# A hybrid diffusion backbone: six pre-norm columns, five staging buffers and another DMA queue in the S5 front, and the first pre-norm pair of the feed-forward stages evacuated ahead of the normed rows

## The chip, the cores and the metric

The kernel runs on one core of a Trainium2 chip. The metric is the device time of one execution in microseconds (us). All other times are read from one execution that the hardware profiler recorded: its span runs from the first to the last instruction, and every time of day below counts from the start of that span.

## What is computed

One inference step of a backbone with two layers over 384 tokens (128 context tokens and 256 latents) of width 1024. A layer is a feed-forward block, a token mixer and another feed-forward block; each sub-layer is modulated by the conditioning and closed by a residual sum and a layer norm:

```
h   = x * (1 + scale) + shift                      # per sub-layer, from the conditioning
ffn = (silu(g) * a) @ w_down,  a, g = split(h @ w_up)      # D_FF = 2816
x   = layer_norm(ALPHA * x + w * gate * sublayer(h))       # w = 1/2 for ffn, 1 for a mixer

s5:  u = h @ w_in;  per group of 16 channels a diagonal complex state of 64, scanned
     forwards and backwards;  y = C s + d_skip * u;  out = a * sigmoid(g) of gelu(y) @ w_glu
```

The mixer of layer 0 is S5, that of layer 1 an RG-LRU block. So there are six sub-layers, numbered 0 to 5: feed-forward (0), S5 (1), feed-forward (2, 3), RG-LRU (4), feed-forward (5).

## The kernel before

Activations are held transposed: 128 channels on the partitions, 384 tokens along the free axis, eight such rows `r[:, k]`. All large products are made in float32 out of rounded parts: a weight tile (`raw`, 128x1024, loaded on the sync engine's queue, SP) is split into `hi` on ScalarE (L252) and `lo` on VectorE (L255), activations likewise into `hh` (L315) and `hl` (L316), and `mm3` (L261) adds three matmuls. Weight tiles have seven buffers, `hi` and `lo` five each, and products six PSUM banks.

**Starting ahead of the norm.** `Norm.add` (L346) gathers the sums of a row and at once writes the row, scaled but not yet normed, to `ph` and `pl`. The next sub-layer begins its products on these "pre-norm" rows. `Norm.pre` (L367) runs them in groups: in the first group, at step k = 4 of 8, TensorE sums the statistics (`stats`, L380), from which GpSimd works out mean and reciprocal deviation in some twenty tiny operations (L394 to L411); in the second group, at step `self.late`, `spread` (L414) broadcasts them with TensorE into `rs` and `ms`. `self.late` is 6 where the sub-layer that was normed is number 1, 2 or 4, that is for the three feed-forward stages 2, 3 and 5, and otherwise 4. Then `pre` loads the weights for what follows and calls `rest` (L425): for each k two operations on VectorE norm the row (L429, L430), `modulate` makes `hh` and `hl` of it, and GpSimd prepares the residual (L432). Everything after that uses normed rows. A product made of pre-norm rows is corrected when it leaves PSUM, by `apply` (L452): a copy of four columns (L455), a product with `rs` (L457) and two additions of `ms` terms (L459).

**Feed-forward** (`ffn`, L467). With a previous norm, the first three pairs (a value and a gate half each, so two PSUM banks a pair, six in all) are pre-norm. They are evacuated by `evac_pre` (L489) after `rest`, in order of the program; the fourth pair is the first on normed rows and needs two of the six banks.

**S5 front** (`s5`, L793). `proj` (L813) makes u = h @ w_in in eight columns of 128 channels. Columns 0 to 3 are pre-norm, in two groups of two; columns 4 to 7 come from normed rows. Each column is corrected, written to a staging buffer `s5stg` (three buffers; VectorE writes the context part, L829, ScalarE the latents, L831 or L833, GpSimd zeroes a separator, L822) and sent to DRAM as `ud` by a DMA on GpSimd's queue (L834), in runs of 49 floats. After every second column two more DMAs on that queue fetch the two columns back into `U` (L838), now with time and channel on the partitions. Columns 4 to 7 are in a part in which GpSimd's work keeps the order of the program.

**What uses U.** `inputs(b)` (L852), for 16 blocks of four groups, multiplies U with the tables `etd` (L864); blocks 2m and 2m + 1 need column m. ScalarE and VectorE copy the results to `s5sb` (L850, L870, L871). The scan (`steps`, L873) is 32 rounds of four small operations (L881 to L884) in three blocks of groups: 0 to 23 on VectorE (needs blocks up to 5), 24 to 39 on GpSimd (up to 9) and 40 to 63 on VectorE, begun after 22 rounds of the first (needs all 16). After it `align` (L894), the output products (L920), a way through DRAM and back into a staging buffer (`fetch`, L927), and the gated projection.

Outside the parts in manual order, the framework orders each engine's work by priority, which is the order of the program, and lets later work that is ready go first where earlier work is not.

Of the kernel before, what the change touches and what calls it, by code (L numbers as in the profile page):

```python
# [7 lines left out]
F32 = mybir.dt.float32  # L8
# [10 lines left out]
N = NP + NS  # L19
# [4 lines left out]
Q = 8  # L24
NC_ = 49
ADA_BUFS = 3
ADA_VEC = [(0, 2, 2)] + [(1, s, kind) for s in range(3) for kind in range(3)]
NX = N + 4
# [5 lines left out]
SK = 0  # L34
ADAS = 4, 2
COLS = ((0, NP, 0), (NP, N, 1))

# [7 lines left out]
def backbone(ctx, tc, a, o):  # L45
    nc = tc.nc
# [237 lines left out]
    def load_singles(srcs):  # L284
        return [stream(src, 1024) for src in srcs]
# [38 lines left out]
    class Norm:  # L324
# [3 lines left out]
        def __init__(self, i):  # L328
# [3 lines left out]
            self.last = []  # L332
            self.late = 6 if i in (1, 2, 4) else 4
            self.st = ExitStack()
# [31 lines left out]

        def pre(self, load, group, srcs, n, then):  # L367


            srcs = [srcs[j:j + n] for j in range(0, len(srcs), n)]  # L370
            w, ps = [load(srcs[0])], []
            for j in range(len(srcs)):
                if j + 1 < len(srcs):
                    w.append(load(srcs[j + 1]))
                ps = ps + group(w[j], NX, self.ph, self.pl, {0: {4: self.stats}, 1: {self.late: self.spread}}.get(j, {}))
            nxt = load(then)
            self.rest()
            return ps, nxt
# [88 lines left out]
    def ffn(i, splits, prev, side, before_last=None, first=None):  # L467
# [31 lines left out]
        with ExitStack() as st:  # L499
            f0 = 0  # L500
            up = lambda f: a["up"][l, s, f]
            for si, nf in enumerate(splits):
                zs.clear()
                f = f0
                if si == 0:
# [6 lines left out]
                    else:  # L512
                        zp = phase(st, f"z{i}")
                        f = 3
                        pss, w = prev.pre(load_pairs, pairs, [up(j) for j in range(f)], 1, [up(f)])
                        for ps in pss:
                            evac_pre(*ps)
# [275 lines left out]
    def s5(i, prev):  # L793
        l, s3 = divmod(i, 3)
        with ExitStack() as st:
# [8 lines left out]
            def stage():  # L804
                return sa.tile([128, Q, NC_], F32, name="s5stg", tag="stg", bufs=3)

# [3 lines left out]
            sin = lambda m: a["s5in"][m // 2, :, (m % 2) * 1024:(m % 2) * 1024 + 1024]  # L810
            nxt = [None]

            def proj(h, pre, before_last=None):  # L813
                if pre:
                    ps, nxt[0] = prev.pre(load_singles, singles, [sin(j) for j in range(4)], 2, [sin(4), sin(5)])
                    nxt.append(load_singles([sin(6), sin(7)]))
                else:
                    ps = singles(nxt[0], N, hh, hl) + singles(nxt[1], N, hh, hl)
                for m in range(4 * h, 4 * h + 4):
                    j = m % 4  # L820
                    stg = stage()
                    G.memset(stg[:, :, 16:17], 0.0)  # L822
                    if pre:
                        t, b = prev.apply(ps[j])
                    else:
                        t, b = ps[j], (0.0, None)
                    inp = t[:, 0:128].rearrange("p (c t) -> p t c", t=Q)
# [4 lines left out]
                    else:  # L832
                        S.activation(stg[:, :, 17:49], ins, AF.Copy)  # L833
                    nc.gpsimd.dma_start(by_channel(ud, m), stg)  # L834
                    if m == 4 * h + 3 and before_last is not None:
                        before_last()
                    for q in ((m - 1, m) if m % 2 else ()):
                        nc.gpsimd.dma_start(U[:, q * 8:q * 8 + 8, :].rearrange("p g c -> p (g c)"), by_place(ud, q))  # L838

            proj(0, True)  # L840
            prev.close()
            with ExitStack() as st2:
# [89 lines left out]
                with tc.manual_schedule(engines={ET.Pool}):  # L932
                    proj(1, False, al_tiles)
                    with tc.manual_schedule(engines={ET.DVE, ET.Activation, ET.SP}):
# [129 lines left out]
    def lru(i, prev):  # L1064
# [88 lines left out]

        ps, w = prev.pre(load_singles, singles, [lin(j) for j in range(4)], 2, [lin(j) for j in range(4, 8)])
        raw = lambda m: fetched(lin(m) if m < 16 else lout(m - 16), 1024)
# [268 lines left out]
```

## Time and profile before

| | us |
|---|---|
| median of 3 runs | 1648.69 (1647.26 to 1650.11) |
| the profiled execution | 1647.38 |
| its span | 1645.6 |
| TensorE busy in the span | 1550.3 (94%) |
| VectorE | 1277.0 (78%) |
| ScalarE | 706.7 (43%) |
| GpSimd | 348.6 (21%) |
| mean granted clock of TensorE | 0.972 of full speed |

PE is TensorE's matmuls and PEld its weight loads, DVE is VectorE, ACT ScalarE, POOL GpSimd, SP the sync engine; a q behind a name is the engine's sequencer or queue. An instruction is named by its line, its operation and "out<-in". Matmuls overlap, so a single one shows about 0.34 us although one ends every 0.175 us or so. Busy shares say how much work an engine has, not what ends last.

### The profile page before, as it was taken

Reading aid. Unit: us, or ns where it says so; the run is one execution under the profiler, and the core shown is the slowest. Engines: PE = TensorE matmul, PEld = TensorE weight load, DVE = VectorE, ACT = ScalarE, POOL = GpSimd, SP = SyncE. Lnnn points to the kernel's source line nnn. Section 1 sums busy time; section 2 is a strip of 40 time slices with the busy share of each in tenths; the row PEclk is TensorE's granted clock in tenths of the full one; section 3 lists DMA queues with packets and bytes.
Section 4 is the critical chain, followed back from the end, with each engine's and each line's share of the span. In section 5 each row is a group of like instructions: output and inputs, shape, how many; then the busy total and the mean of one; then the engine's idle time right before and its main releaser. Section 6 shows DMA issues by size and latency. Waiting matters only on the chain.

```text
span 1645.6 us, 25849 instructions
## 1 busy us (share of the span) xinstructions
PE 1550.3 (94%) x9554; PEld 1475.7 (90%) x9554; DVE 1277.0 (78%) x2742; ACT 706.7 (43%) x1157; POOL 348.6 (21%) x532
## 2 busy tenths in 40 slices
PE   7989999999888999999999999999989599999996
PEld 5877887889877999999999899999977599999995
DVE  4999999977586568968778998977797989644444
ACT  4422332345455456333335533334569366333332
POOL 0145445423562004000001400000155422000001
PEclk9989999999999999999999999999999899999997
DMA  9766777877487642757556266755514143544321
GB/s 351 255 221 213 232 247 233 261 242 262 97 265 239 226 152 79 239 178 247 185 156 223 88 212 201 256 191 167 185 66 135 66 166 120 161 143 141 105 76 39
DMA packets 100863, 301.19 MB, mean 183 GB/s; under 512 B 20320, under 2 KB 32096, under 8 KB 100480
## 3 DMA queue, kind: packets, MB, share of 16 engines
q1 hardware_dynamic: 85792, 249.62, 46.7%
q0 software_dynamic: 13792, 48.31, 9.2%
q8 instruction: 75, 1.23, 0.3%
q10 hardware_dynamic: 1152, 1.61, 0.3%
q14 instruction: 52, 0.43, 0.1%
HBM read 275.89 MB, written 27.80 MB: 185 GB/s over the span
## 4 chain that ended last, share of the span: by engine, by line
PE 68%; DVE 20%; DMA 5%; issue 4%; ACT 2%; POOL 2%; SPq 0%; ACTq 0%; DVEq 0%; POOLq 0%
PE mm L263 21%; PE mm L264 21%; PE mm L265 21%; DVE lo L255 3%; DMA ud<-s5stg 2%; DVE hl L316 1%; DVE r L430 1%; DMA adaw<-in_ada_w 1%; DVE r L429 1%; DVE s5tp L644 1%; DVE lxc L1089 1%; PE mm L920 1%; PE aux L143 1%; PE mm L864 1%; PE aux L387 1%
## 5 line engine op out<-in xcount | busy, mean ns | idle before, releaser
L263 PE MATMUL mm<-hh,hi 128*128 128x384 f32 (+1 forms) x1584 | 550.6, 348 | 25.7 <-DVE w L457 9.2
L264 PE MATMUL mm<-hl,hi 128*128 128x384 f32 (+1 forms) x1584 | 543.5, 343 | 12.7 <-DVE hl L316 12.5
L265 PE MATMUL mm<-hh,lo 128*128 128x384 f32 (+1 forms) x1584 | 542.5, 342 | 0.4 <-DVE lo L255 0.4
L252 ACT ACTIVATE hi<-raw 128x1024 fp32r<-128x1024 f32 (+1 forms) x332 | 322.8, 975 | 487.8 <-PE mm L264 444.1
L255 DVE TENSOR_TENSOR lo<-raw,hi 128x1024 fp32r<-128x1024 f32 (+1 forms) x344 | 393.2, 1148 | 157.7 <-ACT hi L252 146.9
L263 PEld LDWEIGHTS mm<-hh,hi 128*128 128x128 f32 x1584 | 303.5, 192 | 45.9 <-issue 15.0
L264 PEld LDWEIGHTS mm<-hl,hi 128*128 128x128 f32 x1584 | 303.4, 192 | 18.2 <-DVE hl L316 17.6
L265 PEld LDWEIGHTS mm<-hh,lo 128*128 128x128 f32 x1584 | 302.9, 191 | 1.6 <-DVE lo L255 1.4
L263 PE MATMUL mm<-zh,hi 128*128 128x384 f32 x704 | 240.6, 342 | 3.1 <-ACT zh L478 3.1
L264 PE MATMUL mm<-zl,hi 128*128 128x384 f32 x704 | 237.5, 337 | 1.8 <-DVE zl L479 1.6
L265 PE MATMUL mm<-zh,lo 128*128 128x384 f32 x704 | 237.0, 337 | 0.0
L178 DVE SCALAR_TENSOR_TENSOR dump<-raw,cb 128x512 bf16<-128x512 f32 x160 | 110.7, 692 | 47.7 <-DMA raw<-in_ada_t 46.6
L263 PEld LDWEIGHTS mm<-zh,hi 128*128 128x128 f32 x704 | 133.1, 189 | 10.8 <-issue 6.3
L264 PEld LDWEIGHTS mm<-zl,hi 128*128 128x128 f32 x704 | 133.2, 189 | 2.6 <-DVE zl L479 2.6
L265 PEld LDWEIGHTS mm<-zh,lo 128*128 128x128 f32 x704 | 133.2, 189 | 0.0
L478 ACT ACTIVATE zh<-w 128x384 fp32r<-128x384 f32 x88 | 46.1, 524 | 169.0 <-DVE w L486 166.7
L178 DVE SCALAR_TENSOR_TENSOR raw<-raw,cb 128x512 f32<-128x512 f32 x160 | 110.5, 691 | 2.7
L394 POOL TENSOR_TENSOR t<-mv 128x3 f32<-128x3 f32 x5 | 1.9, 380 | 450.0 <-ACT mv L393 450.0
L263 PE MATMUL mm<-ph,hi 128*128 128x388 f32 x208 | 71.2, 342 | 0.0
L264 PE MATMUL mm<-pl,hi 128*128 128x388 f32 x208 | 70.5, 339 | 0.0
L265 PE MATMUL mm<-ph,lo 128*128 128x388 f32 x208 | 70.3, 338 | 0.0
L432 POOL TENSOR_SCALAR r<-r,lag,lab 128x384 f32<-128x384 f32 x40 | 64.5, 1625 | 25.2 <-ACT w L321 25.2
(357 smaller groups left out, 1969.1 us busy)
## 6 DMA issues: line engine op xcount, KB each, us to landing
raw<-in_up SPq DMA_DIRECT2D x176, 512.0 KB, 4.4
raw<-in_ada_t SPq DMA_DIRECT2D x80, 512.0 KB, 4.0
raw<-in_down SPq DMA_DIRECT2D x56, 512.0 KB, 3.8
adaw<-in_ada_w POOLq DMA_DIRECT2D x42, 512.0 KB, 5.3
adaw<-in_ada_w SPq DMA_DIRECT2D x22, 512.0 KB, 7.7
raw<-in_down SPq DMA_DIRECT2D x48, 192.0 KB, 2.4
gd<-s5G POOLq DMA_DIRECT2D x16, 512.0 KB, 4.7
etd<-s5eo POOLq DMA_DIRECT2D x16, 512.0 KB, 5.4
```

The costliest lines, as they stand in the source:

```text
L143: PE.matmul(acc[32 * q:32 * q + 32, :256], cond[:, kh * 4 + q, 6 - 2 * j:38 - 2 * j], w[:, q, :], start=kh == 0, stop=kh == 1, tile_positi ...
L178: V.scalar_tensor_tensor(out, wq, 1.0, cb[:, g, q * 512:q * 512 + 512], op0=OP.mult, op1=OP.mult, accum_out=part[:, t, g, q:q + 1])
L252: S.activation(hi[:, :n], raw[:, :n], AF.Copy)
L255: V.tensor_tensor(lo[:, :n], raw[:, :n], hi[:, :n], op=OP.subtract)
L263: PE.matmul(ps, hi[:, c:c + 128], xh, start=start, stop=False)
L264: PE.matmul(ps, hi[:, c:c + 128], xl, start=False, stop=False)
L265: PE.matmul(ps, lo[:, c:c + 128], xh, start=False, stop=stop)
L316: V.tensor_tensor(hl[:, k, :n], src, hh[:, k, :n], op=OP.subtract)
L387: PE.matmul(st[:, j * 3 + c:j * 3 + c + 1], t[j][:, 128 * c:128 * c + 128], omean, start=False, stop=e == len(terms) - 1 and (j, c) == (1, 2))
L429: V.tensor_tensor(r[:, k, :], r[:, k, :], self.rs, op=OP.mult)
L432: G.tensor_scalar(r[:, k, :], r[:, k, :], lag[:, i, k:k + 1], lab[:, i, k:k + 1], op0=OP.mult, op1=OP.add)
L478: S.activation(zh, z, AF.Copy)
```

## The change

There are three edits. (1) `pre` takes one more argument, `early`, a function that it calls with the products so far, after it has asked for the next weights and before `rest`; and `spread` stands at step 4 for every stage. (2) In the feed-forward stages `early` evacuates the first pre-norm pair; the other two follow after `rest` as before. In the RG-LRU stage `early` does nothing. (3) In the S5 front six columns are pre-norm, in three groups of two, and only columns 6 and 7 use normed rows; columns 0 to 2 are evacuated by `early`, column 3 after `rest`, columns 4 and 5 at the head of the part in manual order; staging has five buffers; the writes to `ud` are issued on ScalarE's queue; the loads of U stay on GpSimd's, four of them (`place`) between the evacuations of columns 5 and 6, four after that of column 7.

```diff
+STG = 5
-            self.late = 6 if i in (1, 2, 4) else 4
-        def pre(self, load, group, srcs, n, then):
+        def pre(self, load, group, srcs, n, then, early):
...
-                ps = ps + group(w[j], NX, self.ph, self.pl, {0: {4: self.stats}, 1: {self.late: self.spread}}.get(j, {}))
+                ps = ps + group(w[j], NX, self.ph, self.pl, {0: {4: self.stats}, 1: {4: self.spread}}.get(j, {}))
             nxt = load(then)
+            early(ps)
             self.rest()
...
-                        pss, w = prev.pre(load_pairs, pairs, [up(j) for j in range(f)], 1, [up(f)])
-                        for ps in pss:
+                        pss, w = prev.pre(load_pairs, pairs, [up(j) for j in range(f)], 1, [up(f)],
+                                          lambda pss: evac_pre(*pss[0]))
+                        for ps in pss[1:]:
                             evac_pre(*ps)
...
-                return sa.tile([128, Q, NC_], F32, name="s5stg", tag="stg", bufs=3)
+                return sa.tile([128, Q, NC_], F32, name="s5stg", tag="stg", bufs=STG)
...
-            def proj(h, pre, before_last=None):
-                if pre:
-                    ps, nxt[0] = prev.pre(load_singles, singles, [sin(j) for j in range(4)], 2, [sin(4), sin(5)])
-                    nxt.append(load_singles([sin(6), sin(7)]))
-                else:
-                    ps = singles(nxt[0], N, hh, hl) + singles(nxt[1], N, hh, hl)
-                for m in range(4 * h, 4 * h + 4):
-                    j = m % 4
+            def proj(ms, ps, pre):
+                for m, p in zip(ms, ps):
...
-                    nc.gpsimd.dma_start(by_channel(ud, m), stg)
-                    if m == 4 * h + 3 and before_last is not None:
-                        before_last()
-                    for q in ((m - 1, m) if m % 2 else ()):
-                        nc.gpsimd.dma_start(U[:, q * 8:q * 8 + 8, :].rearrange("p g c -> p (g c)"), by_place(ud, q))
-
-            proj(0, True)
+                    nc.scalar.dma_start(by_channel(ud, m), stg)
+
+            def place(ms):
+                for m in ms:
+                    nc.gpsimd.dma_start(U[:, m * 8:m * 8 + 8, :].rearrange("p g c -> p (g c)"), by_place(ud, m))
+
+            ps, nxt = prev.pre(load_singles, singles, [sin(j) for j in range(6)], 2, [sin(6), sin(7)],
+                               lambda ps: proj(range(3), ps, True))
+            proj((3,), ps[3:4], True)
...
-                    proj(1, False, al_tiles)
+                    proj((4, 5), ps[4:], True)
+                    place(range(4))
+                    proj((6, 7), singles(nxt, N, hh, hl), False)
+                    al_tiles()
+                    place(range(4, 8))
```

## Rows read from the trace of the kernel before

**Rows 1.** The page, the chain that ended last, shares of the span by line.
```profile
PE mm L263 21%; PE mm L264 21%; PE mm L265 21%; DVE lo L255 3%; DMA ud<-s5stg 2%; DVE hl L316 1%; DVE r L430 1%; DMA adaw<-in_ada_w 1%; DVE r L429 1%; DVE s5tp L644 1%; DVE lxc L1089 1%; PE mm L920 1%; PE aux L143 1%; PE mm L864 1%; PE aux L387 1%
```

**Rows 2.** The same chain in order of time, 385 to 485: start, duration, what.
```profile
421.46 8.60 DMA ud<-s5stg
...
458.85 6.76 DMA s5U<-ud
465.65 10.27 PE mm L864 x68
...
477.93 0.26 DVE w L881
```

**Rows 3.** Waits, 390 to 480: who waited for whom, us in total, times, longest.
```profile
POOL s5U L838 <- DMA ud<-s5stg: 26.0, 6, 7.3
...
DVE s5stg L829 <- DMA ud<-s5stg: 15.0, 5, 5.5
...
DVE w L881 <- ACT s5sb L850: 3.5, 1, 3.5
```

**Rows 4.** Timeline of VectorE and ScalarE: start, us, engine, line, operation, count [idle before].
```profile
406.02 1.50 DVE L429 TENSOR_TENSOR r<-r,rs 128x384 f32<-128x384 f32 x3 [2.65 <-ACT rs L423]
...
423.34 1.01 DVE L457 TENSOR_TENSOR w<-mm,rs 128x384 f32<-128x384 f32 x2
424.27 0.74 DVE L459 SCALAR_TENSOR_TENSOR w<-ms,gw,w 128x128 f32<-128x128 f32 x2
424.92 0.33 DVE L829 TENSOR_SCALAR s5stg<-w,gw 128x128 f32<-128x128 f32 x1
...
425.04 0.78 ACT L831 ACTIVATE s5stg<-w,gw 128x256 f32<-128x256 f32 x1 [1.06 <-DVE w L459]
...
648.88 1.22 DVE L255 TENSOR_TENSOR lo<-raw,hi 128x1024 fp32r<-128x1024 f32 x1
```

**Rows 5.** Timeline of TensorE, rows with idle time before them.
```profile
422.57 0.44 PE L264 MATMUL mm<-hl,hi 128*128 128x384 f32 x1 [1.78 <-DVE hl L316]
...
637.67 0.41 PE L263 MATMUL mm<-hh,hi 128*128 128x384 f32 x1 [1.89 <-DVE w L457]
...
1353.60 0.33 PE L421 MATMUL aux<-ident,sthi 128*128 128x128 f32 x1 [0.79 <-POOL sthi L410]
```

**Rows 6.** Stretches: length, busy us (count) by engine, granted clock, DMA share, GB/s.
```profile
638.00:645.00 7.00, 6.21 (x21) 5.69 (x20) 7.00 (x17) 4.49 (x9) 4.04 (x5) 0.51 0.00 0
...
1354.00:1366.00 12.00, 11.65 (x70) 11.65 (x71) 11.17 (x26) 9.30 (x22) 7.51 (x5) 1.00 0.15 50
```

**Rows 7.** DMAs from issue to landing, lines L834 (`ud`), L838 (`U`), L925 (ScalarE's queue).
```profile
DMA to landing us min/median/max: 5.6/7.3/11.4
...
DMA to landing us min/median/max: 3.0/4.8/6.8
...
DMA to landing us min/median/max: 4.6/5.5/7.2
```

**Rows 8.** Timeline of GpSimd, 395 to 480.
```profile
414.25 0.63 POOL L845 DMA_DIRECT2D s5init<-in_s5s  x1
...
462.89 0.43 POOL L881 TENSOR_TENSOR s5p<-a,s5sb 128x64 f32<-128x64 f32 x1
```

**Rows 9.** Timeline of TensorE and VectorE, 432 to 480: input matmuls, first scan step.
```profile
433.58 3.34 PE L864 MATMUL mm<-s5U,s5e 128*128 128x128 f32 x28
...
445.04 14.04 PE L864 MATMUL mm<-s5U,raw 128*128 128x128 f32 x124
...
450.53 0.26 DVE L881 TENSOR_TENSOR w<-a,s5sb 128x96 f32<-128x96 f32 x1
```

**Rows 10.** Stretches, line L881 alone (one per scan round): VectorE and GpSimd.
```profile
451.00:460.00 9.00, 2.57 (x10) 0.00 (x0) 1.00 1.05 213
467.00:476.00 9.00, 2.17 (x6) 2.24 (x7) 0.79 0.64 181
```

**Rows 11.** Timeline of GpSimd, 905 to 911: the end of the statistics.
```profile
908.50 1.25 POOL L411 TENSOR_TENSOR stlo<-yn,sthi 128x6 fp32r<-128x6 f32 x1
```

More of the change, by code (lines that the diff above doesn't have):

```diff
@@ L810, in s5 @@
             sin = lambda m: a["s5in"][m // 2, :, (m % 2) * 1024:(m % 2) * 1024 + 1024]
-            nxt = [None]
-            def proj(h, pre, before_last=None):
-                if pre:
-                    ps, nxt[0] = prev.pre(load_singles, singles, [sin(j) for j in range(4)], 2, [sin(4), sin(5)])
-                    nxt.append(load_singles([sin(6), sin(7)]))
-                else:
-                    ps = singles(nxt[0], N, hh, hl) + singles(nxt[1], N, hh, hl)
-                for m in range(4 * h, 4 * h + 4):
-                    j = m % 4
+            def proj(ms, ps, pre):
+                for m, p in zip(ms, ps):
                     stg = stage()
@@ L823, in proj @@
                     if pre:
-                        t, b = prev.apply(ps[j])
+                        t, b = prev.apply(p)
                     else:
-                        t, b = ps[j], (0.0, None)
+                        t, b = p, (0.0, None)
                     inp = t[:, 0:128].rearrange("p (c t) -> p t c", t=Q)
@@ L1152, in two @@
             return [split_raw(x, 1024, E) for x in raws]
-        ps, w = prev.pre(load_singles, singles, [lin(j) for j in range(4)], 2, [lin(j) for j in range(4, 8)])
+        ps, w = prev.pre(load_singles, singles, [lin(j) for j in range(4)], 2, [lin(j) for j in range(4, 8)],
+                          lambda ps: None)
         raw = lambda m: fetched(lin(m) if m < 16 else lout(m - 16), 1024)
```

## The prediction

> **What bounds the kernel now.** I read the chain that ended last first, by line, because busy shares can't price a change in one stage: most of it is the three matmul lines of the weight streams, 63%, which the change doesn't touch; but 2% of the span, more than 30 us, is one transfer, `ud<-s5stg` [rows 1]. Next, the same chain in order of time around the S5 front [rows 2]. From 421.5 to 465.6 us it is five DMAs, one behind the other, with next to nothing computed in between: four writes of staging buffers to DRAM (the first is shown), then the load of the last part of U. After it come the last input matmuls, then scan steps on VectorE from 477.9.
>
> Why the writes are in series is in the waits of that stretch [rows 3]: VectorE waits 15.0 us for a staging buffer (three of them, eight columns), and GpSimd waits 26.0 us for writes to land before it may issue loads; the next write stands behind that load on the same queue. A second cause: the first write goes out at 421.5, although the normalisation factors were there when VectorE started on `r` at 406.0 [rows 4]. GpSimd, which issues it, first had its eight operations of L432 to do, paced by the normed rows.
>
> For the feed-forward part I read where TensorE sits idle at the start of the first normed pair: 1.89 us in the first of the three stages (shown), 2.18 and 2.17 in the others, ended by L457, which reads the first pre-norm pair and so frees its PSUM banks [rows 5]. Then the granted clock [rows 6]: the next 7 us run at 0.51 of full speed, so at the 1.2 GHz level; after waits of 0.79 and 0.42 us at 1353 it stays at 1.00. One stall so costs its own 2 to 3 us and some 3.4 us of matmuls at half speed, about 6 us in each stage.
>
> **The change, S5 front.** Evacuating one pre-norm column costs VectorE 0.47 (half of L457's pair), 0.65 to 0.74 (two of L459) and 0.33 (L829), 1.5 us, and ScalarE 0.78 (L831) [rows 4]. Three columns and the split of the last weights, 5.6 us, now stand ahead of the normed rows; about 3.8 us of that stood between them already, so the last row comes some 2 to 3 us later than 422.4, at about 425. That is covered: `spread` ended at 406.0, 24 matmuls of its group follow at 0.175 us (70 in 12 us [rows 6]), to 410.2, and now a third pre-norm group of 48, so normed matmuls start at 418.6 and want the last row at 426.0. If the cover fails, each microsecond is one of TensorE; the kernel before paid 1.78 us at such a row [rows 5]. TensorE ends the projection at 427.0 instead of 433.5.
>
> The first write goes out at 408.5, the next two by 412.5, 9 to 13 us earlier, and no write stands behind a load. Issuing eight on ScalarE costs it some 0.35 us each, 3 us, of which one half falls among the rows, inside the 2 to 3 us above. How long a write of these short rows takes to land on ScalarE's queue is not shown: the nearest are 5.5 us there for longer rows and 7.3 us for these rows on GpSimd's [rows 7]; I take 6. New waits: the write of column 6 stands on ScalarE behind its memset, which is on GpSimd behind the load of column 3, whose write is issued after the rows (425.5) and lands near 432; so ScalarE's first scan-input copies come at 433. Until then TensorE has banks for four blocks, and six copies of 0.85 us fit before block 5 is due.
>
> The loads stay on GpSimd. They can go out in gaps between the L432s, as the load at 414.25 did [rows 8], at about 417, or only behind them, at about 425; with 4.8 us to land [rows 7], U's first part is there between 423 and 430. Input matmuls start between 427.0 and 430, against 433.58, and don't stop for U again. Eight blocks ran in 14.04 us [rows 9], 1.76 each; block 5 is through 10.5 us after the start and its copies 2 us later. The scan's first step, at 450.53 before [rows 9], comes at 439.5 to 442.5, or up to 446 if the clock falls at the start; I take 441.5, 9 us earlier. The last inputs are done by 460, so VectorE's wait of 3.5 us for them [rows 3] goes too. Against that, GpSimd's own scan block starts at about 449 instead of 462.89 [rows 8] and slows VectorE sooner: a round of four steps takes 0.92 us alone (ten in 9 us) and 1.34 beside it (seven in 9 us on GpSimd) [rows 10]. Before it were some 13.4 rounds alone and 8.6 beside, 23.9 us; then 8 and 14, 26.1 us. The third block so starts at 467.6 instead of 477.93, and its tail stays about as long. What follows waits for that tail, so the gain is carried on: **10 us**, with ends of 5 (inputs at 430 and the low clock) and 13 (inputs at 427).
>
> **The change, feed-forward.** The first pair's evacuation, about 3.6 us of VectorE, moves ahead of the rows, and `spread` comes two steps of 1.05 us earlier. Nothing is added. The bank wait goes. What is late next: first `spread`. In the second stage GpSimd's chain ends at 909.75 [rows 11] and TensorE would be there at 907.3, so it waits 2.4 us; in the third it waits 1.2 now [rows 5] and will wait 3.3; in the first 0.5. Second, the split of the fourth pair's weights (L255 at 648.88 to 650.10 [rows 4]), behind the other evacuations on a VectorE that is busy 7.00 of 7 us [rows 6]. Before, TensorE reached that pair at 650.2, since the third ran at the low clock. Now it would be there at 644.7, and the split, with a wait of 1.45 us of VectorE gone, at about 648.4. So the stage is bound by VectorE, and of 6 us at most 1 to 3 can be had: in the first stage 2 us if the clock holds, minus 1.5 if it falls; in the second 2.7 or minus 0.7; in the third 2.2 or minus 1.2. I take **2.5 us** for the three together, with ends of plus 7 and minus 3.5.
>
> Here rows bear on a rule that speaks against this part. The wait of 2 us let the clock fall and those of 0.79 and 0.42 did not [rows 5, 6]. The Trainium skill (TensorE: Matmul & The Clock Gate, Part 1) has the low clock as the default, which only activity releases, whatever the idleness comes from. By that rule a stall that only changes its place pays the low clock again: the feed-forward term would be a loss of 3.5 us instead of a gain of 2.5, which is the first rival.
>
> **Sum.** 10 + 2.5 = 12.5 us. The profiled execution took 1647.38 (span 1645.6 and 1.8 around it), so 1634.9; the median of the runs stands 1.3 above it, so **1636.2 us**.
>
> **Rivals.** (1) *The stall moves.* The waits at `spread` and at the fourth pair's split let the clock fall as before. For it: VectorE has no slack there [rows 6]; against: the waits are 1.7 to 3.3 us, some in two pieces. Feed-forward minus 3.5, S5 10: 6.5 us, 1642.2. (2) *U comes no earlier.* GpSimd holds the loads until its L432s are through, these are later because the rows are, and TensorE starts the inputs at the low clock after 3 us of idleness. For it: GpSimd works in order; against: an init load slipped in between [rows 8]. S5 5, feed-forward 0: 1643.7. (3) *Slower.* The earlier `spread` decides: TensorE waits for GpSimd's chain in all three stages, the clock falls there and again at the fourth pair (3.4 us each time, and a wait of 3), about 5 us net a stage after what the bank wait gives back, 15 in all. It turns the sign once the three lose more than S5's 10. For it: that chain stretches when VectorE is busy (one of its last steps took 1.25 us, where others take 0.2 [rows 11]); against: two such waits at 1353 cost no clock. 1648.7 + 5 = 1653.7. (4) *The evacuation isn't first after all*, because the scheduler orders it otherwise: feed-forward 0, S5 10, which is inside the forecast.
>
> **How the numbers follow.** Forecast 0.53 (1631 to 1640, with rival 4), stall moves 0.23, U no earlier 0.12, slower 0.06, and 0.06 for both parts at their good ends (13 and 7 us, 1628.7). A measurement of this kernel tells about 0.2%, 3.3 us, from no change. Faster by more than that: 0.53, 0.06, most of rival 1 (0.19) and nearly half of rival 2 (0.05), together 0.83; within it 0.11; slower 0.06. The range leaves out the best end and the last of rivals 2 and 3: 1629.5 to 1645.0.
>
> **What would show it.** Right: the first `ud<-s5stg` near 408 to 410 and no wait of GpSimd for one of more than 3 us; input matmuls from 427 to 430 in one stretch; the first scan step near 441, the last near 502 instead of 512.6; L457 no longer ending a wait of TensorE in the feed-forward stages. The feed-forward term is wrong if TensorE waits at `spread` or for L255 and the clock shows 0.5 behind it; the S5 term is wrong if GpSimd's first load is after 426, or if normed rows hold up the last two columns.

## The result: 1632.6 us, about 1% below

The median after the change is 1632.64 us (1628.45 to 1633.9, four runs), beside 1648.13 for the kernel before: a ratio of 0.990, with a 95% interval of 0.9878 to 0.9921. The forecast was 1636.2, faster. The profiled execution took 1631.38, its span 1629.6.

All stages are compared by one landmark: the twelve matmuls that sum a norm's statistics (L387 before, L388 after; the change shifts lines). The first two numbers of time are the first start and the last end. Before, for the norms that open S5, feed-forward 2, feed-forward 3, RG-LRU, feed-forward 5 and the end:

```profile
L387 PE MATMUL aux<-omean,sum x12: 250/250/271, 394.8 to 396.0; 128*128 128x1 f32 x12
L387 PE MATMUL aux<-omean,sum x12: 250/250/271, 611.6 to 612.9; 128*128 128x1 f32 x12
L387 PE MATMUL aux<-omean,sum x12: 250/250/271, 897.4 to 898.7; 128*128 128x1 f32 x12
L387 PE MATMUL aux<-omean,sum x12: 250/250/271, 1184.0 to 1185.2; 128*128 128x1 f32 x12
L387 PE MATMUL aux<-omean,sum x12: 250/250/271, 1340.6 to 1341.9; 128*128 128x1 f32 x12
L387 PE MATMUL aux<-omean,sum x12: 250/250/271, 1623.9 to 1625.1; 128*128 128x1 f32 x12
```

After:

```profile
L388 PE MATMUL aux<-omean,sum x12: 250/250/271, 393.4 to 394.6; 128*128 128x1 f32 x12
L388 PE MATMUL aux<-omean,sum x12: 250/250/271, 600.4 to 601.6; 128*128 128x1 f32 x12
L388 PE MATMUL aux<-omean,sum x12: 250/250/271, 882.6 to 883.9; 128*128 128x1 f32 x12
L388 PE MATMUL aux<-omean,sum x12: 250/250/271, 1168.9 to 1170.1; 128*128 128x1 f32 x12
L388 PE MATMUL aux<-omean,sum x12: 250/250/271, 1326.3 to 1327.6; 128*128 128x1 f32 x12
L388 PE MATMUL aux<-omean,sum x12: 250/250/271, 1607.9 to 1609.2; 128*128 128x1 f32 x12
```

Differences of neighbours are the lengths of the stages. S5 fell from 216.8 to 207.0, so 9.8 us; the feed-forward stages from 285.8, 286.6 and 283.3 to 282.2, 286.3 and 281.6, so by 3.6, 0.3 and 1.7, together 5.6. RG-LRU is 0.8 longer, and 1.4 us came ahead of S5, where nothing was edited: that stretch ended between 391.9 and 397.3 in the traces of this study.

**S5 after.** First the waits of 390 to 480, as in [rows 3], then DMA issues on ScalarE's queue (ACTq) and GpSimd's, then the consumers:

```profile
POOL s5U L833 <- DMA ud<-s5stg: 14.9, 5, 3.9
```

```profile
407.72 0.40 ACTq L829 DMA_DIRECT2D ud<-s5stg  x1
```

```profile
413.91 0.62 POOL L833 DMA_DIRECT2D s5U<-ud  x1 [0.37 <-issue]
...
430.21 0.59 POOL L833 DMA_DIRECT2D s5U<-ud  x1 [2.41 <-DMA ud<-s5stg]
```

```profile
425.80 7.25 PE L861 MATMUL mm<-s5U,s5e 128*128 128x128 f32 x64
...
438.57 5.44 PE L861 MATMUL mm<-s5U,raw 128*128 128x64 f32 x32 [2.36 <-DMA s5U<-ud]
...
440.97 0.26 DVE L878 TENSOR_TENSOR w<-a,s5sb 128x96 f32<-128x96 f32 x1
...
451.11 0.44 POOL L878 TENSOR_TENSOR s5p<-a,s5sb 128x64 f32<-128x64 f32 x1 [5.55 <-ACT s5sb L847]
```

Three writes leave ahead of most of the rows (the third at 413.05) and three loads (413.91, 417.65 and 421.49) go out before or between GpSimd's row operations; the waits for writes are 14.9 us instead of 26.0, none over 3.9. VectorE's waits for a buffer are gone. Input matmuls start at 425.8 instead of 433.58 [rows 9], the scan's first step at 441.0 instead of 450.53, and GpSimd's own scan block at 451.11 instead of 462.89 [rows 8].

**Feed-forward after.** First, from before, the other waits of TensorE in the three fronts (in total, times, longest; the waits at `spread` in the third stage, 0.79 and 0.42 us, come on top), and the granted clock of the second and third stage (the column after POOL's busy time):

```profile
PE mm L263 <- DVE w L457: 2.7, 2, 1.9
PE mm L263 <- DVE w L457: 3.2, 2, 2.2
PE mm L263 <- DVE w L457: 2.6, 2, 2.2
```

```profile
925.00:932.00 7.00, 6.16 (x20) 6.16 (x21) 6.67 (x18) 3.73 (x7) 1.50 (x3) 0.53 0.01 2
1369.00:1376.00 7.00, 6.55 (x22) 6.04 (x22) 7.00 (x19) 4.10 (x8) 2.04 (x3) 0.55 0.16 66
```

After: TensorE's rows with idle time before them, all that the three stages' fronts have, then stretches with the granted clock:

```profile
635.35 0.45 PE L266 MATMUL mm<-hh,lo 128*128 128x384 f32 x1 [1.65 <-DVE lo L256]
...
893.75 0.33 PE L422 MATMUL aux<-ident,sthi 128*128 128x128 f32 x1 [1.03 <-POOL sthi L411]
895.01 0.33 PE L422 MATMUL aux<-ident,stlo 128*128 128x128 f32 x1 [0.94 <-POOL stlo L412]
...
920.06 0.44 PE L266 MATMUL mm<-hh,lo 128*128 128x384 f32 x1 [2.07 <-DVE lo L256]
...
1339.23 0.33 PE L422 MATMUL aux<-ident,sthi 128*128 128x128 f32 x1 [2.82 <-POOL sthi L411]
...
1364.90 0.45 PE L266 MATMUL mm<-hh,lo 128*128 128x384 f32 x1 [0.88 <-DVE lo L256]
```

```profile
632.00:640.00 8.00, 6.35 (x36) 6.03 (x35) 8.00 (x18) 4.97 (x9) 0.69 (x2) 1.00 0.32 84
...
921.00:925.00 4.00, 4.00 (x16) 4.00 (x15) 4.00 (x5) 0.49 (x1) 0.00 (x0) 0.57 0.74 265
...
1341.00:1345.00 4.00, 4.00 (x15) 4.00 (x15) 4.00 (x11) 2.05 (x5) 0.00 (x0) 0.57 0.14 51
```

The bank wait of [rows 5] is gone from all three. In its place stand waits at `spread` and for `lo` of the second normed pair, 1.65, 4.04 and 3.70 us in the three stages. The clock, at half for 7 us before in each stage ([rows 6] and above), stays at 1.00 in the first; in the other two it drops to the 1.2 GHz level for most of the 4 us shown, in the second behind the wait for `lo`, in the third behind the wait at `spread`.

So the stall moved, and it hardly shrank: TensorE idles 9.7 us in the three fronts before (2.7, 3.2 and 3.8) and 9.4 after. What changed is the clock. It is at half for some 6.8 us in each stage before and for 3.4 us in two stages after; a microsecond at half speed loses half, so about 10 us against 3.4, less 1 us because TensorE idled in part of the low stretches of before. That makes some 6 us with the change in idle time, an estimate from these rows, beside the 5.6 of the stages.

### The profile page after: what moved, and what is told of

The parts are those of the page before. It is cut to its first block, busy times and chain, and to the rows that moved or that the text cites. A ratio compares the mean times of both kernels' runs of the same rounds, so it can differ in the third digit from the quotient of the medians.

```text
span 1629.6 us, 25853 instructions
## 1 busy us (share of the span) xinstructions
PE 1546.1 (95%) x9554; PEld 1474.6 (90%) x9554; DVE 1278.5 (78%) x2750; ACT 709.4 (44%) x1157; POOL 336.5 (21%) x524
## 4 chain that ended last, share of the span: by engine, by line
PE 70%; DVE 20%; DMA 3%; issue 3%; ACT 3%; POOL 1%; SPq 0%; ACTq 0%; DVEq 0%; POOLq 0%
PE mm L264 22%; PE mm L266 22%; PE mm L265 22%; DVE lo L256 2%; DVE hl L317 1%; PE aux L144 1%; DMA adaw<-in_ada_w 1%; DVE s5sb L881 1%; DVE w L878 1%; DVE w L460 1%; ACT w L322 1%; DVE lxc L1090 1%; PE mm L917 1%; DVE s5sb L880 1%; DVE w L879 1%
## 5 line engine op out<-in xcount | busy, mean ns | idle before, releaser
L264 PE MATMUL mm<-hh,hi 128*128 128x384 f32 (+1 forms) x1568 | 542.1, 346 | 14.5 <-DVE hh L1143 7.3
L265 PE MATMUL mm<-hl,hi 128*128 128x384 f32 (+1 forms) x1568 | 535.7, 342 | 10.2 <-DVE hl L317 10.1
L266 PE MATMUL mm<-hh,lo 128*128 128x384 f32 (+1 forms) x1568 | 535.4, 341 | 5.0 <-DVE lo L256 5.0
L264 PEld LDWEIGHTS mm<-hh,hi 128*128 128x128 f32 x1568 | 298.7, 191 | 32.9 <-issue 15.7
L265 PEld LDWEIGHTS mm<-hl,hi 128*128 128x128 f32 x1568 | 299.0, 191 | 13.3 <-DVE hl L317 12.7
L266 PEld LDWEIGHTS mm<-hh,lo 128*128 128x128 f32 x1568 | 298.6, 190 | 7.0 <-DVE lo L256 7.0
L264 PE MATMUL mm<-ph,hi 128*128 128x388 f32 x224 | 77.4, 346 | 0.0
L265 PE MATMUL mm<-pl,hi 128*128 128x388 f32 x224 | 76.6, 342 | 0.0
L266 PE MATMUL mm<-ph,lo 128*128 128x388 f32 x224 | 76.3, 341 | 0.0
L545 DVE SCALAR_TENSOR_TENSOR r<-mm,gate,r 128x128 f32<-128x128 f32 (+1 forms) x144 | 53.2, 410 | 20.5 <-PE mm L266 20.5
```

The lines of the kernel that those rows point to most:

```text
L264: PE.matmul(ps, hi[:, c:c + 128], xh, start=start, stop=False)
L265: PE.matmul(ps, hi[:, c:c + 128], xl, start=False, stop=False)
L266: PE.matmul(ps, lo[:, c:c + 128], xh, start=False, stop=stop)
L545: V.scalar_tensor_tensor(r[:, m, c0:c1], ps[:, c0:c1], gate[:, m, g:g + 1], r[:, m, c0:c1], op0=OP.mult, op1=OP.add)
```

## Experiments

Stage lengths from each trace, and the ratio to runs of the kernel before on the same chip. Before's own median was 1648.1 us beside the first row of after and 1642.9, 1644.7 or 1642.3 beside the others, so only ratios are compared; times worked out from them use 1645. Each row of stages is one execution; that of before is the profiled one of 1647.38 us.

| kernel | S5 | ff 2 | ff 3 | ff 5 | ratio (95%) |
|---|---|---|---|---|---|
| before | 216.8 | 285.8 | 286.6 | 283.3 | 1 |
| after | 207.0 | 282.2 | 286.3 | 281.6 | 0.990 (0.9878 to 0.9921) |
| after again | 207.0 | 283.1 | 288.3 | 281.4 | 0.9938 (0.9918 to 0.9958) |
| S5 part alone | 206.7 | 286.1 | 286.8 | 283.3 | 0.9952 (0.9938 to 0.9967) |
| feed-forward part alone | 215.0 | 282.2 | 286.4 | 281.3 | 0.9988 (0.9976 to 1.0) |
| before, writes on ScalarE | 214.6 | 286.5 | 286.7 | 283.3 | 0.998 (0.9968 to 0.9993) |
| after, writes on GpSimd | 215.3 | 282.3 | 286.7 | 281.4 | 0.9979 (0.9962 to 0.9996) |
| after, three buffers | 205.8 | 282.3 | 284.7 | 281.4 | 0.992 (0.9896 to 0.9945) |
| after, column 3 early | 206.0 | 282.3 | 286.3 | 281.6 | 0.9894 (0.9876 to 0.9913) |
| after, spread at 6 | 208.9 | 287.0 | 285.8 | 285.5 | 0.9974 (0.9963 to 0.9985) |
| after, no pair early | 208.3 | 284.3 | 284.3 | 281.2 | 0.9918 (0.9901 to 0.9934) |
| after, split ahead | 204.6 | 280.3 | 285.5 | 280.2 | 0.9876 (0.9858 to 0.9893) |
| split ahead, spread at 5 | 205.8 | 280.3 | 282.3 | 280.3 | 0.9905 (0.9878 to 0.9933) |
| split ahead, column 3 early | 204.2 | 280.9 | 284.0 | 278.9 | 0.990 (0.9876 to 0.9925) |

Without any edit in it, S5 took 215.0 and 216.8; among the kernels with the whole S5 part it took 204.6 to 208.9 (column 3 early not counted). So a difference of 2 us in that column alone says nothing, and one of 4 little. In the feed-forward columns, kernels without an edit there (S5 part alone; before, writes on ScalarE) sum to 856.2 and 856.5 beside before's 855.7, but after itself to 850.1 and 852.8.

### The two parts, each alone

The S5 part alone is edit (3) with `early` doing nothing in the feed-forward stages and `late` kept. The feed-forward part alone is edits (1) and (2).

> The S5 front of the change alone; feed-forward stages as before (spread at step 6, all three pre-norm pairs evacuated after the rows). By the landmarks of the two traces (the statistics of sub-layer 1 come 11.2 us earlier after the change, those of sub-layer 0 already 1.4) the S5 part is worth 9.8 us: 1638.3, and the three feed-forward stages take as long as before. Rival, the stall moved and the feed-forward part gave nothing: then this kernel takes as long as the changed one, 1632.6.

> The feed-forward part alone on the kernel before: first pre-norm pair evacuated ahead of the rows and spread at step 4. By the landmarks it is worth 3.6, 0.3 and 1.7 us in the three stages, 5.6 together: 1642.5. By the prediction's own term 2.5: 1645.6. By its first rival (stall and low clock only change their place) a loss of 3.5: 1651.6.

S5 alone: 0.9952, 7.9 us (5.4 to 10.2), and 10.1 us in its stage. Feed-forward alone: 0.9988, 2.0 us (0 to 3.9), though its three stages are 5.8 us shorter in the trace; why the median shows less is open. The trace of before is of an execution some 4 us above the median of before on this chip, and the stretch ahead of S5, in which nothing is edited, moves by more than that difference. So S5 carries most of the gain.

> The kernel after the change, unaltered, on the same chip and beside the same runs of the kernel before as the three that follow. So far it stood at 0.990 of before (about 16 us), while its two parts alone gave 7.9 us (S5) and 2.0 us (feed-forward), and another kernel with spread at step 4 stood at 0.992 on their chip. Theory 1 (the parts add up): the ratio comes out near 0.993 to 0.994, 10 to 12 us below before. Theory 2 (together they give more than alone): 0.990 again, 16 us; by the traces' statistics matmuls S5 gave 9.8 and the three feed-forward stages 5.6 us.

0.9938: 10.2 us (6.9 to 13.5), where the first comparison gave 16; the parts add up to 9.9. The two intervals meet only between 0.9918 and 0.9921. The size of the gain is thus known to be 10 to 16 us, no closer; by all stages from S5 on it is 14.6 in the first trace of after and 12.2 in the second.

### S5: the queue or the columns?

```diff
-                    nc.gpsimd.dma_start(by_channel(ud, m), stg)
+                    nc.scalar.dma_start(by_channel(ud, m), stg)
```

> The kernel before with one edit: the writes of the staging buffers are issued on ScalarE's queue instead of GpSimd's. Four pre-norm columns, three staging buffers, spread and the feed-forward stages as before. Theory 1 (writes and loads in series on one queue are the cause): the four writes no longer stand behind loads, the first leaves near 412, the scan's first step comes 5 to 8 us earlier than the 450.5 of before and the time falls by 5 to 8 us, most of what the whole S5 part gave (8 to 10). Theory 2 (that only four columns were pre-norm, so half of the columns wait for the normed rows, is the cause): columns 4 to 7 are computed when they were, the first scan step comes at most 3 us earlier and the time falls by 0 to 3 us.

> The kernel after the change with one edit undone: the writes of the staging buffers go back to GpSimd's queue; six pre-norm columns and five buffers stay. Theory 1 (the queue is the cause): the writes of columns 0 to 2 are late behind GpSimd's eight operations on the normed rows, those of columns 6 and 7 stand behind four loads, and the scan's first step is 5 us or more later than after's 441.0; 4 to 8 us above after's time. Theory 2 (the columns are the cause): with three writes ahead of the rows and the loads ordered behind six columns, little stands in series even on one queue; 0 to 3 us above after's time.

Neither theory holds alone. The queue without the columns gives 3.3 us (1.2 to 5.3). The columns without the queue give 3.5 us together with the feed-forward part, which has 2.0 of it, so 1 to 2, which these intervals don't tell from nothing. Together they give 8. The stages say the same: 214.6 and 215.3, where kernels without any edit in S5 have 215.0 and 216.8, against 207.0. First the kernel before with its writes on ScalarE: the first write and the first scan step.

```profile
422.28 0.39 ACTq L834 DMA_DIRECT2D ud<-s5stg  x1
...
449.13 0.26 DVE L881 TENSOR_TENSOR w<-a,s5sb 128x96 f32<-128x96 f32 x1
```

The queue is free, but nothing is there to be written: the columns are evacuated behind the rows. The first scan step comes 55.6 us after the statistics (393.5), before 55.7. Then the kernel after with its writes on GpSimd:

```profile
430.69 0.89 POOL L829 DMA_DIRECT2D ud<-s5stg  x1 [0.77 <-ACT s5stg L828]
431.57 2.17 POOL L833 DMA_DIRECT2D s5U<-ud  x4
```

```profile
438.30 2.04 PE L861 MATMUL mm<-s5U,s5e 128*128 128x128 f32 x8 [10.85 <-issue]
```

Now three columns are in DRAM early, and it is of no use: GpSimd keeps the order of the program, the first loads stand behind the writes of columns 4 and 5, which wait for these columns, which wait for the rows. All four loads go out at 431.57, where after has its first three at 413.9 to 421.5, and TensorE stands for 10.85 us before the first input matmul. This is the outcome of rival 2 of the prediction, made by one line; the loads are held by the writes ahead of them, though, and not by GpSimd's row operations, as that rival had it.

```diff
-STG = 5
+STG = 3
```

> The kernel after the change with three staging buffers instead of five. Theory 1 (the buffers matter little once writes start at 408): column 3's evacuation at 424 finds the first buffer long free (its write, issued at 407.7, had landed by 414), only columns 6 and 7 may wait for the writes of columns 3 and 4, landing near 430 and 434; within 2 us of after's time. Theory 2 (the buffers are what lets the last columns leave): the writes of columns 6 and 7 go out 4 us or more later, their loads as well, the GpSimd block of the scan (needs column 4 and 5) and the third block (columns 6, 7) start later, and 2 to 5 us come back.

0.992, beside 0.9938 for after on that chip, and a stage of 205.8: the buffers are not what gained.

```diff
-                               lambda ps: proj(range(3), ps, True))
-            proj((3,), ps[3:4], True)
+                               lambda ps: proj(range(4), ps, True))
```

> The kernel after the change, with column 3 of the S5 front evacuated ahead of the normed rows too, like columns 0 to 2. In the trace of after, the odd blocks' last input matmuls read the start of the next column (blocks 4 and 5 need columns 2 and 3), and column 3's load landed last of those, at 438.5, since its write went out at 425.2, behind the rows; the first scan step was at 441.0, 47.6 us after the statistics matmuls. Theory 1 (column 3's late write gates the scan): its write goes out before 415, TensorE has no wait for a part of U before block 6, the first scan step comes 44 to 46 us after the statistics, the S5 stage (statistics to statistics, 207.0 in after) is 2 us shorter, the time 1 to 3 us below after's. Theory 2 (the rows are what is tight): VectorE spends 1.5 us more ahead of the rows, TensorE waits 1 to 2 us for hh or hl of a normed row and the clock may fall there; the stage is as long as after's or up to 3 us longer.

Of theory 1 the end of the stop came true, of both theories the rest is too small to tell. Input matmuls, in two rows without a stop, and the first step (the statistics here start at 397.3):

```profile
431.40 7.25 PE L860 MATMUL mm<-s5U,s5e 128*128 128x128 f32 x64
438.49 21.66 PE L860 MATMUL mm<-s5U,raw 128*128 128x128 f32 x192
...
444.00 0.26 DVE L877 TENSOR_TENSOR w<-a,s5sb 128x96 f32<-128x96 f32 x1
```

TensorE no longer waits for U. The inputs start 34.1 us after the statistics, not 32.4 as in after, and TensorE waits 0.52 us for a normed row at 423.19; but in the repeated run of after they start at 34.5, so that the edit makes the rows late isn't shown. The first step is at 46.7, in the two runs of after at 47.6 and 47.7; 1 us is left, and the ratio doesn't tell it from after's.

### Feed-forward: the pair or spread?

After with `lambda pss: None` and all three pairs evacuated behind the rows, `spread` at 4; and after with the pair early and `spread` back at 6 in the three stages:

> The changed kernel with the evacuations of all three pre-norm pairs after the rows, as before, but spread at step 4. If the early evacuation is the part that gains in the feed-forward stages, the bank wait of some 2 us and the low clock behind it are back in each stage, with the waits at spread on top in the second and third: 6 to 9 us more than the changed kernel, 1639 to 1642. If the earlier spread is what gained, it takes 1632.6 to 1635.

> The changed kernel with spread back at step 6 in the feed-forward stages; the early evacuation stays. If the earlier spread is what costs the second and third stage (waits of 2.0 and 2.8 us at spread there, and the low clock behind each), these waits go to 0 and about 1, the low clock behind spread goes, and the kernel takes 2 to 5 us less than 1632.6. If VectorE bounds these stretches whatever TensorE does (the split for the second normed pair ends last), it takes the same within 1.5 us, and TensorE waits longer or shorter for that split by what it no longer waits at spread.

The first took its second branch, the second missed with both, and that is the main finding here. Without the early pair the stages sum to 849.8, as after's 850.1, and the ratio is as good. With the early pair and `spread` at 6 they sum to 858.3, 2.6 more than before's 855.7, and the time is some 9 us above that of the other kernel of this pair (0.9974 against 0.9918, same chip). The S5 part alone, measured on the same chip, has neither edit (0.9952): beside it the earlier `spread` gives 5.6 us, with intervals that lie apart, and the early pair costs 3.6 us, with intervals that just overlap. So what gained is `spread`. First the kernel with `spread` at 6, then that with no pair early, in feed-forward 2:

```profile
641.29 0.45 PE L266 MATMUL mm<-hh,lo 128*128 128x384 f32 x1 [3.64 <-DVE lo L256]
```

```profile
639.19 0.45 PE L266 MATMUL mm<-hh,lo 128*128 128x384 f32 x1 [2.05 <-DVE lo L256]
```

In the second the bank wait is gone although the first pair is evacuated behind the rows, as before: VectorE's whole block starts earlier, the first pair's products are read 23.8 us after the statistics instead of 25.4, and TensorE doesn't stop for its banks. In the first the bank wait is gone too, but the block is as late as before and the wait has moved to `lo`.

That is so in feed-forward 2. In feed-forward 3 `spread` at 4 doesn't start the block earlier: GpSimd's chain ends no sooner, and VectorE's first row operation comes 13.7 us after the statistics in the kernel with no pair early as in before. There TensorE waits 0.97 and 1.00 us at `spread` and 1.66 us for `lo` where it waited 3.2 us for banks, and the stage is 2.3 us shorter because the clock stays at 1.00 in that trace. In feed-forward 5 the block starts 0.6 us earlier, the waits are 3.3 us instead of 3.8, and the clock is at half for 3.4 us instead of 6.8.

That `lo` is bound by the order on VectorE, not by its work, is shown by asking for the second normed pair's weights before the third pre-norm pair is evacuated:

```diff
-                        for ps in pss[1:]:
-                            evac_pre(*ps)
+                        evac_pre(*pss[1])
+                        ahead.append(load_pairs([up(f + 1)]))
+                        evac_pre(*pss[2])
...
-                    w = load_pairs([up(f)])
+                    w = ahead.pop() if ahead else load_pairs([up(f)])
```

> The kernel after the change, with the weights of the second normed pair of each feed-forward stage asked for (and so split on VectorE and ScalarE) before the third pre-norm pair is evacuated, not after it. In after TensorE waited for lo of that pair 1.65, 2.07 and 0.88 us in the three stages, and about 3.4 us at half the clock followed in the last two. Theory 1 (only the order on VectorE is wrong; the third pair's banks are not wanted so early): the waits for lo go, what is left are the waits at spread (0, 2.0 and 2.8), the time is 3 to 7 us below after's. Theory 2 (VectorE is the bound of this stretch whatever the order): the wait comes back one pair later, as a wait for the third pair's banks or for the next lo, of about the same size; within 2 us of after's time.

All waits for `lo` are gone in the three stages and none came in their place (the expectation put low clock behind two of these waits; in feed-forward 5 of after it stood behind the wait at `spread`); the pair's two splits start 25.5 and 31.8 us after the statistics instead of 33.7 and 36.6, and the stages sum to 846.0, 4.1 below after's. The ratio, 0.9876, is the best of all, beside 0.9894 for the column 3 kernel on that chip, whose feed-forward stages are after's: about 3 us, at the low end of what theory 1 gave, with intervals that overlap. In feed-forward 2, from 632 to 640, TensorE is busy 8.00 of 8 us, in after 6.35 (this stage runs 2.2 us ahead of after's).

```diff
-1: {4: self.spread}
+1: {5 if self.i in (1, 2, 4) else 4: self.spread}
```

> The kernel with the second normed pair's weights asked for before the third pre-norm pair's evacuation, and spread in the feed-forward stages at step 5 instead of 4. In that kernel at step 4 TensorE waits only at spread, 0, 2.0 and 2.5 us in the three stages. Theory 1 (GpSimd's chain of tiny operations ends at a fixed time after the statistics, so one step of 1.05 us later saves that much waiting, and VectorE has room for it): 0, 1.0 and 1.5 us of waiting left, 1 to 3 us below the kernel at step 4. Theory 2 (VectorE starts its 16 row operations from spread and everything behind it is late by as much): waits for lo or for the first normed pair's banks come back, the time is the same or up to 4 us above.

> Both edits together: the second normed pair's weights asked for before the third pre-norm pair's evacuation, and column 3 of the S5 front evacuated ahead of the rows. Alone the first gave 4 us in the median (1.9, 0.8 and 1.4 us in the three stages of its trace) and the second 1.0 us in its S5 stage and nothing that the medians tell. Theory 1 (they touch different stages and add up): at or up to 2 us below the kernel with the first alone, S5 stage 205 to 206 us. Theory 2 (the second costs as much through later rows as it gives): the same time as the first alone, or up to 2 us above.

Spread at 5 takes one of the two waits out of feed-forward 3 (1.0 us left) and leaves the 2.6 of feed-forward 5; no bank wait or `lo` wait returns. Its stages sum to 842.9, those of the kernel with both edits to 843.8. In time (0.9905 and 0.990, after itself 0.9938 beside them) the two can't be told apart, nor from split ahead alone; they are some 5 to 6 us below after, with intervals that still touch its own.

## The prediction, step by step

**S5, forecast 10 us.** 9.8 in the stage in both runs of after, 7.9 alone by the medians, so the sum held. Of its steps: the first write was put at 408.5 and left at 407.72, the third at 412.5 and 413.05; the projection was to end at 427.0 and did at 425.8, and 1.4 of that is the earlier start of the stage. The first step was put at 441.5, the third block at 467.6 and the scan's end at about 502; they came at 441.0, 465.05 and 500.77; from first step to third block are 24.1 us and not 26.1, and GpSimd's block, which slows VectorE, began at 451.11 and not at 449. The longest wait of GpSimd for a write was 3.9 us, over the 3 that the prediction named. No normed row held up TensorE in this trace, though in the repeated run of after one did, for 1.89 us at 430.33: the cover is as thin as its numbers said.

Two steps inside were wrong, and offset each other. First, U was to be read without a stop. TensorE waited 2.36 and 0.73 us for it, and behind the first wait the clock was at 0.50 from 440.4 to 443.4. That blocks 2m and 2m + 1 need column m, as stated ahead of the prediction, is not the whole of it: an odd block's last matmuls also read the start of the next column, so block 5 and, in this trace, with it the scan's start wait for column 3's load. Its write goes out behind the rows, at 425.19, and the chain of work that ended last runs through it:

```profile
425.19 4.49 DMA ud<-s5stg
...
430.21 8.31 DMA s5U<-ud
438.57 0.67 PE mm L861 x4
```

Second, a load was priced at 4.8 us and a write at 6. This load took 8.31, and the medians after are 6.6 and 8.0. They were made up for by the inputs' start: 425.8, or 427.2 with the 1.4 us by which the stage began earlier, is the early end of the forecast's 427 to 430. (The row read as eight blocks in 14.04 us holds 124 of their 128 matmul records, so a block takes 1.81 us and not 1.76, which is 0.3 us up to block 5.) In the two kernels with column 3 early TensorE doesn't stop for U, in all eight others with the S5 part and its writes on ScalarE it does; what the stop costs isn't shown, since the first step, 46.7 and 46.6 us after the statistics in the two, lies among the 45.4 to 48.7 of the eight. Why loads land later is open.

**Feed-forward, forecast 2.5 us.** 5.6 in the stages, 2.0 alone by the medians: inside plus 7 to minus 3.5. What was late next was named rightly: `spread` was to wait 0.5, 2.4 and 3.3 us in the first, second and third of the stages and did 0, 1.97 and 2.82, and then came `lo`. (The prediction calls it the fourth pair's split; it is the fifth pair's, the second on normed rows.) The mis-sized term is that split. By the prediction it would end 36.8 us after the statistics (648.4 less 611.6; 650.10 less the 1.45 would be 648.65) and TensorE arrive at 33.1. TensorE did arrive at 33.3, but the split ended at 34.9:

```profile
612.54 1.01 DVE L458 TENSOR_TENSOR w<-mm,rs 128x384 f32<-128x384 f32 x2
...
634.08 1.21 DVE L256 TENSOR_TENSOR lo<-raw,hi 128x1024 fp32r<-128x1024 f32 x1
```

VectorE's block starts 12.1 us after the statistics, where before its first row operation started at 625.19, so at 13.6. The working took VectorE's wait of 1.45 us off and left out that an earlier `spread` starts the whole block 1.5 us earlier in this stage. So the wait was 1.65 us and not 3.7, the clock held, and the stage gave 3.6 where 2 was the good case.

The prediction gave one price to two edits and named a sign of being wrong: a wait at `spread` or for the split with the clock at 0.5 behind it. That sign came, in the second and the third stage. Either edit alone ends the bank wait, as the prediction said of both; but the order of the evacuation, by itself, gains no time, and the earlier `spread` gains all of it. And it gains through the clock and not through less waiting, 9.4 us of it beside 9.7, so part of the 5.6 us is chance: in the repeated run of after the three stages gave 2.9, with the clock at half for 6.8 us in the second.

**Rivals.** The first, the stall moves, was half right: waits of 1.65, 4.04 and 3.70 us stand where the waits of before are 2.7, 3.2 and 3.8, as it said, but the clock fell in two stages of three and for about half the time. The rule named beside it (the Trainium skill, TensorE: Matmul & The Clock Gate, Part 1: the low clock is the default, and activity releases it) would have all three stages pay; the trace agrees in the second and third and not in the first, where a wait of 1.65 us left the clock at 1.00. The outcome of the second is what one line back on GpSimd's queue makes. The third, slower, had its waits at `spread` in the second and third stage, but no stage paid the low clock twice: in the second it fell behind `lo` alone, in the third behind `spread` alone.

**Range.** 1629.5 to 1645.0 held 1632.6. The medians of the same kernel in two comparisons are 1632.64 and 1631.28, while before's differ by 6 us; so the forecast gain of 12.5 us lies between the 16 and 10.2 that were measured, and how near it came can't be said more closely.

## What to carry to other kernels

A queue that is kept in order is priced by what stands behind its waiting instructions, not by its issue time: moving the writes paid only since the data was there early as well, and having the data early paid only since the loads no longer stood behind later writes; each half alone gave 1 to 3 us by the medians, of 8 to 10 for both. Where one engine is busy from a broadcast to the next consumer, bring the broadcast forward first, and then put its work in the order in which consumers need it: a split moved ahead of an evacuation that nobody waited for shortened the three stages by another 4.1 us in the trace. A wait that goes can come back elsewhere: count the idle time of the whole front, and the time at the low clock apart from it. Two edits in one diff are priced apart, even where they seem to serve one end.

## What the runs showed of the hardware

**Issue and landing.** A write of these short rows costs GpSimd 0.89 to 1.0 us to issue and ScalarE 0.37 to 0.40, but in the median it lands no sooner: 6.8 us on GpSimd's queue and 8.0 on ScalarE's. After with its writes on GpSimd, then after:

```profile
L829 POOL DMA_DIRECT2D ud<-s5stg x8: 885/904/997, 409.5 to 435.5; - x8
DMA to landing us min/median/max: 4.9/6.8/9.5
```

```profile
L829 ACTq DMA_DIRECT2D ud<-s5stg x8: 366/367/402, 407.7 to 431.9; - x8
...
DMA to landing us min/median/max: 4.5/8.0/12.6
```

The Trainium skill (Trainium Kernel Development and Optimization, Key Constraints) says that issuing from several engines only saves issue time. Eight times 0.54 us is 4.3; the stage differs by 8.3 between these two kernels, with a scatter of up to 4, and the median landing was no faster, for the loads neither (6.6 and 6.8 us). The rest is put down to loads that no longer wait in order behind writes, by the rows at 431.57 and 438.30 above.

**The same waits, another clock.** In feed-forward 3 of the kernel with the split ahead, two waits at `spread` are followed by a low clock:

```profile
889.59 0.33 PE L422 MATMUL aux<-ident,sthi 128*128 128x128 f32 x1 [0.97 <-POOL sthi L411]
890.92 0.33 PE L422 MATMUL aux<-ident,stlo 128*128 128x128 f32 x1 [1.00 <-POOL stlo L412]
```

```profile
890.00:898.00 8.00, 7.08 (x27) 7.08 (x28) 6.07 (x14) 2.41 (x5) 0.86 (x1) 0.58 0.38 131
```

In the kernel with no pair early, two waits of the same length in the same place are not:

```profile
899.08 0.33 PE L422 MATMUL aux<-ident,sthi 128*128 128x128 f32 x1 [0.97 <-POOL sthi L411]
900.40 0.33 PE L422 MATMUL aux<-ident,stlo 128*128 128x128 f32 x1 [1.00 <-POOL stlo L412]
```

```profile
900.00:908.00 8.00, 7.60 (x47) 7.60 (x48) 6.55 (x14) 5.71 (x13) 3.98 (x3) 1.00 0.35 126
```

With the split ahead and `spread` at 5, and one wait, the clock held and the stage took 282.3 instead of 285.5. So part of what a stage gives differs from trace to trace with the clock, and a forecast of one stage can't be closer than some 3 us here.
